# Attention's queries by rotated rows of all heads in one tile, and a norm's row spread by a repeated column

## The chip, the cores and the metric

The kernel runs on one core of a Trainium2 chip. Time is that of the device in microseconds, from the launch to the end on that core. The engines are named as the profile does: PE is TensorE (PEld its weight loads), DVE is VectorE, ACT is ScalarE, POOL is GpSimd, SP is SyncE, which issues nearly all transfers.

## The reference, cut to what matters

The network has two blocks of two layers each, on 512 tokens of width 1024, in float32. Only the first block's token mixer is touched. Each of its two layers projects the tokens into four branches (a short convolution, a gated linear attention, a latent attention and a 31-tap convolution), normalises and joins them. The latent attention computes its queries so:

```python
qm = (rms_norm(cq, g_mla_q) @ w_mla_uq).reshape(bsz, s, MLA_HEADS, MLA_NOPE + MLA_ROPE)
q_c = jnp.concatenate([qm[..., :MLA_NOPE], apply_rope(qm[..., MLA_NOPE:], cos, sin)], axis=-1)
...
k_rope = jnp.broadcast_to(apply_rope(kr[:, :, None, :], cos, sin), (bsz, s, MLA_HEADS, MLA_ROPE))
k_c = jnp.concatenate([kvm[..., :MLA_NOPE], k_rope], axis=-1)

def apply_rope(x, cos, sin):
    x1, x2 = xf[..., :half], xf[..., half:]
    return jnp.concatenate([x1 * c - x2 * s, x1 * s + x2 * c], axis=-1)
```

There are 4 heads, each with 64 plain and 32 rotated columns; the query latent has 256 columns, the key latent 128. The 31-tap branch ends in a layer norm over 256 channels.

## The kernel before, in words

Activations in the mixer lie feature-major: 128 features on the partitions, 512 tokens along a row. Large matmuls are made of three products of float32r halves (`mm3`, lines 368 to 370): weights arrive by transfer as `raw`, ScalarE casts their high half `hi` (line 374), VectorE subtracts it to give `lo` (line 376), and TensorE multiplies hi by hi, hi by lo and lo by hi. Small matmuls, the queries and the scores among them, are plain float32.

`mixers_` loads the layer's constants, projects the latents `cq` (two tiles), `ckv` and `kr`, and in layer 0 makes the angle table `self.trig` (`angles`, lines 580 to 612: integer positions, range reduction on VectorE, a sine on ScalarE, a sign on VectorE). The table holds cosines on partitions 64 to 95 and signed sines on 96 to 127. Lines 709 to 711 rotate the keys' shared row `kr` with it. Layer 1 uses the same table.

Then `merge` interleaves four generators, each with a weight of its own: `linear` (the gated linear attention; its masks are line 923), `mla` (the latent attention), `convolutions` (first the remaining projections of the layer, then 60 multiply-adds per layer in line 784, then a layer norm) and `output`. The program order so written goes to a planner, which simulates a time line with costs of its own and writes each engine's instruction order from it; each engine then runs its own list in order, and waits on semaphores.

`feat_rsqrt` is used for three norms per layer: of `cq`, of `ckv` (both in `mla`, lines 1048 and 1052), and in the 31-tap branch (line 798). `feat_r` gets one number per token: squares, TensorE's sums with a column of ones (line 562), VectorE's scale (line 383), and GpSimd's power (line 384). The four columns `r[:, t]` have tokens on partitions; to spread them along a row over all partitions, VectorE scales the identity's rows by a column (line 573, a diagonal, tile `d`, two buffers) and TensorE multiplies a matrix of ones by it (line 574).

`queries(h)` makes one head's tile from the 128 columns of its weights, which `layout` has put as 64 plain, 32 rotated and the same 32 with their halves exchanged: two matmuls of K = 128 into one PSUM bank (line 1070), a ScalarE copy of the 64 plain rows into `Q` (line 1071), and three VectorE operations on 32 partitions: the rotated rows by the cosines (line 1073), the exchanged rows by the sines (line 1074), and their sum (line 1075). `keys(h)` makes two heads' keys and copies `kr` under each (lines 1081 and 1082). The scores (line 1095) read rows 0 to 95 of `Q` and `K`.

Of the kernel before, what the change touches and what calls it, by code (L numbers as in the profile page):

```python
# [11 lines left out]
F32 = mybir.dt.float32  # L12
# [4 lines left out]
OP = mybir.AluOpType  # L17
# [4 lines left out]
S = 512  # L22
# [33 lines left out]
def stack(units):  # L56
    return np.stack(units)


def cols(v):  # L60

    return v.reshape(-1, 128).T


def rng(a, n):
    return list(range(a, a + n))


def layout(i):
# [11 lines left out]
    for l in range(2):  # L81
        w = f("w_in")[l]
        o = {}
        at = 0
        for n, s in zip(("b", "c", "h", "gq", "gk", "gv", "gg", "gf", "gb", "cq", "ckv", "kr", "cfm"),
                        (256, 256, 256, 128, 128, 256, 256, 16, 16, 256, 128, 32, 512)):
            o[n] = at
            at += s
        kr = rng(o["kr"], 32)
        fm = lambda a: fm_unit(w, rng(a, 128))  # L90
        gvgg = w[:, o["gv"]:o["gv"] + 512]
        units = [fm_unit(w, rng(o["gf"], 32) + [-1] * 32 + kr + kr[16:] + kr[:16]), fm(o["gq"]),
                 fm(o["gk"]), fm(o["cq"]), fm(o["cq"] + 128), fm(o["ckv"])]
        units += [fm(o["cfm"]), fm(o["cfm"] + 256), fm(o["cfm"] + 128), fm(o["cfm"] + 384)]
        units += [tok_units(gvgg, 0, kp) for kp in range(4)]
        for c in range(2):
            units += [fm(o["c"] + 128 * c), fm(o["h"] + 128 * c), fm(o["b"] + 128 * c)]
        A[f"win{l}"] = stack(units)
        uq = f("w_mla_uq")[l]
        q = []  # L100
        for h in range(4):
            r = rng(96 * h + 64, 32)
            q += rng(96 * h, 64) + r + r[16:] + r[:16]
        uq = uq.reshape(2, 128, 384)[:, :, q].reshape(2, 128, 4, 128).transpose(1, 2, 0, 3).reshape(128, 1024)
        kv = f("w_mla_ukv")[l].reshape(128, 4, 128)
        ukv = np.zeros((128, 1024), kv.dtype)
        ukv[:, :256] = kv[:, :, :64].reshape(128, 256)
        ukv[:, 256:512] = kv[:, :, 64:].reshape(128, 256)
        A[f"wmla{l}"] = stack([uq, ukv])
        up = f("w_gla_a_up")[l]  # L110
        wu = np.zeros((32, 256), up.dtype)
        wu[:16, :128] = up[0]
        wu[16:, 128:] = up[1]
        A[f"wgla{l}"] = wu
        wo = f("w_out")[l]
        A[f"wout{l}"] = stack([tok_units(wo, c, kp) for p in ((0, 3), (1, 2)) for c in range(2) for kp in p])
        wup = f("w_ffn_up")[l]
        A[f"wup{l}"] = stack([fm_unit(wup, rng(h * FF + 128 * m, 128)) for m in range(FT) for h in range(2)])
        wd = f("w_ffn_down")[l]
        units, k0 = [], 0  # L120
        for n in FFN_PARTS:
            units += [tok_units(wd, c, kp) for c in range(2) for kp in range(k0 // 2, (k0 + n) // 2)]
            k0 += n
        A[f"wdown{l}"] = stack(units)
        v = [cols(f("b_gla_a")[l].reshape(-1))]
        for c in range(2):
            v.append(f("w_sc_conv")[l][:, 128 * c:128 * c + 128].T)
        v += [cols(f("g_mla_q")[l]), cols(f("g_mla_kv")[l])]
        for c in range(2):
            v.append(f("w_cfm_dw")[l][:, 128 * c:128 * c + 128].T)  # L130
        v += [cols(f("g_cfm_ln")[l]), cols(f("b_cfm_ln")[l]), cols(f("g_branch")[l])]
        v.append(f("w_ffn_dw")[l].reshape(3, 44, 128).transpose(2, 1, 0).reshape(128, 132))
        A[f"vec{l}"] = np.concatenate(v, 1)
        A[f"gh{l}"] = f("g_gla_head")[l][None]
# [4 lines left out]
    for l in range(2):  # L139
        w = f("w_in_2")[l]  # L140
        b = f("b_in_2")[l]
        o = {}
# [117 lines left out]
class Lane:  # L260
# [20 lines left out]
    def s(self, shape, dt=F32):  # L281
        n = int(np.prod(shape[1:]))
        return self.tile(shape, dt, *(("s16", 12) if n <= 16 else ("s64", 4)))

    def d(self):
        return self.tile((128, 128), F32, "d", 2)


class Net:
# [276 lines left out]
    def feat_rsqrt(self, L, sq, n):  # L566

        nc = self.nc
        r = self.feat_r(L, sq, n)
        R = L.P()  # L570
        for t in range(NT):
            d = L.d()
            nc.vector.tensor_scalar(d, self.ident, r[:, t:t + 1], None, op0=OP.mult)
            nc.tensor.matmul(R[:, t * 128:(t + 1) * 128], self.ones, d, start=True, stop=True)
        return R

    def square(self, L, src):
# [63 lines left out]

    def block1_consts(self):
        self.gmask = self.blk.tile([128, 8, 128], U8, name="gmask")
        self.trig = self.blk.tile([128, S], F32, name="trig1")
        self.hmask = self.const("hmask", 256, self.blk)

    def mixers(self, l, x):
# [3 lines left out]
    def mixers_(self, l, x):  # L651
        nc = self.nc
        ve, ac = nc.vector, nc.scalar
        A = Lane(self, "A", ps=2)
        G = Lane(self, "G", ps=2, w=5, v=11)
        M = Lane(self, "M", ps=2, w=7, v=5)
# [18 lines left out]
        ps = fst[0]  # L675
        ga = G.w()
        ac.copy(ga[0:32], ps[0:32])
        kr = M.w()
# [11 lines left out]
        q, k = G.w(), G.w()  # L690
        ps = fst[1]
        ac.activation(q, ps, AF.Copy, scale=32 ** -0.5)
        ps = fst[2]
# [6 lines left out]
        latent = ac.copy(ckv, self.fm(A, st.next(), x))  # L700

        with self.tc.issue_after(last.ins):
            if l == 0:
                raw = self.rawp.tile([128, 1024], F32, tag="raw", name=self.nm("raw"))
                nc.sync.dma_start(raw, self.A["gmask"])
                nc.gpsimd.tensor_copy(self.gmask.rearrange("p a b -> p (a b)"), raw)
                self.angles(M, "pos", 0, 1, 2, self.trig, latent)
            tmp = M.w()
            ve.tensor_tensor(out=tmp[64:96], in0=kr[96:128], in1=self.trig[96:128], op=OP.mult)
            ve.tensor_tensor(out=kr[64:96], in0=kr[64:96], in1=self.trig[64:96], op=OP.mult)  # L710
            ve.tensor_tensor(out=kr[64:96], in0=kr[64:96], in1=tmp[64:96], op=OP.add)

        gv = [G.v() for _ in range(NT)]
# [331 lines left out]
    def mla(self, L, wm, cq, ckv, kr, g_q, g_kv, attended):  # L1045
        nc = self.nc
        ve, ac = nc.vector, nc.scalar
        R = self.feat_rsqrt(L, [self.square(L, a) for a in cq], 256)
# [3 lines left out]
        R = self.feat_rsqrt(L, [self.square(L, ckv)], 128)  # L1052
        ve.scalar_tensor_tensor(ckv, ckv, g_kv, R, op0=OP.mult, op1=OP.mult)
        yield 1
        Q, K = self.g8(), self.g8()
        T = self.trig
        v = []
        for t in range(NT):
            ps = L.P((128, 256))
# [3 lines left out]
            v.append(vt)  # L1063
        yield 1

        def queries(h):
            ps = L.P()
            for k in range(2):
                o = (2 * h + k) * 128
                nc.tensor.matmul(ps, wm[:, 0, o:o + 128], cq[k], start=k == 0, stop=k == 1)  # L1070
            ac.copy(Q[0:64, h], ps[0:64])
            tmp = L.w()
            ve.tensor_tensor(out=Q[64:96, h], in0=ps[64:96], in1=T[64:96], op=OP.mult)
            ve.tensor_tensor(out=tmp[64:96], in0=ps[96:128], in1=T[96:128], op=OP.mult)
            ve.tensor_tensor(out=Q[64:96, h], in0=Q[64:96, h], in1=tmp[64:96], op=OP.add)

        def keys(h):
            ps = L.P()
# [5 lines left out]
        for h in (0, 2):  # L1084
            keys(h)
            yield 1
        for h in range(4):
            queries(h)
            yield 1.7
        PP, PT, O = {}, {}, {}  # L1090

# [1032 lines left out]
```

## Time and profile before

| | |
|---|---|
| time, median of 3 runs (lowest, highest) | 2965.17 us (2964.11, 2965.36) |
| profiled execution: its time, its span | 2962.75 us, 2960.6 us |
| mean granted TensorE clock over the span | 0.983 |
| busy share of the span: PE, DVE, ACT, POOL | 97%, 73%, 48%, 13% |

The profiled execution is one run of its own; the span runs from its first to its last instruction, and the time has some 2 us more around it. The granted clock is a share of TensorE's full 2.4 GHz; 0.5 is its lower level, 1.2 GHz, and a stretch's figure is the mean over it. Busy times of TensorE come from modelled ends of pipelined matmuls.

### The profile page before, as it was taken

The numbers are of one execution on the slowest core, as the hardware profiler recorded it, in microseconds if no ns is written. First come the engines' busy times: TensorE is split into PE (matmuls) and PEld (weight loads), VectorE is DVE, ScalarE is ACT, GpSimd is POOL, SyncE is SP. The second block draws the span as 40 slices with busy tenths as digits, with TensorE's granted clock in tenths as the row PEclk, the third lists the DMA queues.
The fourth block names the chain that finished last, engine by engine and source line by source line (L and its number), as shares of the span: only waits on it lengthen the run. The fifth ranks groups of instructions, "written<-read, shape, count | busy, mean of one in ns | idle before, by whom it ended". The sixth has DMA issues, their size and how long they took to land.

```text
span 2960.6 us, 37914 instructions
## 1 busy us (share of the span) xinstructions
PE 2864.5 (97%) x13982; PEld 2246.9 (76%) x13982; DVE 2167.0 (73%) x3532; ACT 1430.1 (48%) x2214; POOL 372.2 (13%) x359
## 2 busy tenths in 40 slices
PE   7999999999999999999999998999999999989996
PEld 6777888878778888878787786777687777867774
DVE  6998655576978556687876447999768764479997
ACT  4444423335444333335544424888445444238884
POOL 1012000010011000011101002110411011021203
PEclk9999999999999999999999998999999999989998
DMA  5121332332213233343232266999632322669993
GB/s 194 54 90 51 93 97 95 100 128 89 65 58 94 94 99 100 107 154 110 61 97 89 76 253 235 380 384 358 233 92 66 98 76 81 226 240 371 387 381 122
DMA packets 128589, 457.34 MB, mean 154 GB/s; under 512 B 15696, under 2 KB 16912, under 8 KB 126992
## 3 DMA queue, kind: packets, MB, share of 16 engines
q1 hardware_dynamic: 117776, 425.50, 41.5%
q0 software_dynamic: 7168, 16.79, 1.7%
q10 hardware_dynamic: 3456, 12.58, 1.1%
q8 instruction: 112, 1.84, 0.3%
q14 instruction: 77, 0.63, 0.1%
HBM read 429.12 MB, written 27.26 MB: 154 GB/s over the span
## 4 chain that ended last, share of the span: by engine, by line
PE 86%; DVE 10%; ACT 2%; issue 1%; DMA 0%; POOL 0%; POOLq 0%; SPq 0%; DVEq 0%; ACTq 0%
PE AP L368 16%; PE AP L369 16%; PE AP L370 16%; PE HP L370 4%; PE HP L369 4%; PE HP L368 4%; PE BP L370 3%; PE BP L368 3%; PE BP L369 3%; PE YP L370 2%; PE YP L369 2%; PE YP L368 2%; DVE cacc L784 2%; DVE lo L376 2%; PE O L1610 1%
## 5 line engine op out<-in xcount | busy, mean ns | idle before, releaser
L368 PE MATMUL AP<-g,hi 128*128 128x512 f32 (+1 forms) x1856 | 717.8, 388 | 9.7 <-DVE g L886 4.0
L369 PE MATMUL AP<-g,hi 128*128 128x512 f32 (+1 forms) x1856 | 710.8, 383 | 10.6 <-DVE g L376 10.6
L370 PE MATMUL AP<-g,lo 128*128 128x512 f32 (+1 forms) x1856 | 710.7, 383 | 0.0
L376 DVE TENSOR_TENSOR lo<-raw,hi 128x1024 fp32r<-128x1024 f32 x326 | 412.2, 1266 | 359.7 <-ACT hi L374 350.3
L374 ACT CAST hi<-raw 128x1024 fp32r<-128x1024 f32 x326 | 341.8, 1050 | 562.6 <-PE AP L369 380.7
L368 PEld LDWEIGHTS AP<-g,hi 128*128 128x128 f32 x1856 | 353.2, 191 | 80.4 <-DVE g L886 4.9
L369 PEld LDWEIGHTS AP<-g,hi 128*128 128x128 f32 x1856 | 353.6, 191 | 77.6 <-DVE g L376 12.0
L370 PEld LDWEIGHTS AP<-g,lo 128*128 128x128 f32 x1856 | 353.4, 190 | 66.1 <-issue 1.4
L376 DVE TENSOR_TENSOR lo<-g,hi 128x1024 fp32r<-128x1024 f32 x204 | 239.2, 1219 | 23.3 <-ACT hi L374 22.9
L374 ACT CAST hi<-g 128x1024 fp32r<-128x1024 f32 x204 | 207.0, 1051 | 50.2 <-PE AP L370 32.4
L376 DVE TENSOR_TENSOR lo<-wide,hi 128x1024 fp32r<-128x1024 f32 x180 | 212.3, 1225 | 25.1 <-ACT hi L374 23.5
L370 PE MATMUL HP<-hi,Txt 128*96 128x512 f32 x512 | 203.8, 398 | 0.0
L369 PE MATMUL HP<-lo,Txt 128*96 128x512 f32 x512 | 203.2, 397 | 0.2
L368 PE MATMUL HP<-hi,Txt 128*96 128x512 f32 x512 | 200.9, 400 | 1.1 <-ACT Txt L374 1.1
L374 ACT CAST hi<-wide 128x1024 fp32r<-128x1024 f32 x180 | 182.7, 1050 | 21.9 <-PE HP L370 18.7
L368 PE MATMUL AP<-hi,g 128*128 128x512 f32 x400 | 165.8, 418 | 0.3 <-DVE g L886 0.3
L370 PE MATMUL AP<-hi,g 128*128 128x512 f32 x400 | 158.1, 397 | 0.4 <-DVE g L891 0.4
L369 PE MATMUL AP<-lo,g 128*128 128x512 f32 x400 | 157.4, 394 | 0.0
L368 PE MATMUL BP<-hi,g 128*128 128x512 f32 x352 | 136.8, 390 | 0.0
L369 PE MATMUL BP<-lo,g 128*128 128x512 f32 x352 | 136.6, 389 | 0.0
L370 PE MATMUL BP<-hi,g 128*128 128x512 f32 x352 | 134.0, 389 | 0.0
L369 PEld LDWEIGHTS HP<-lo,Txt 128*96 128x96 f32 x512 | 83.4, 163 | 39.2 <-DVE lo L376 2.6
(509 smaller groups left out, 4901.7 us busy)
## 6 DMA issues: line engine op xcount, KB each, us to landing
wide<-in_wmoeu SPq DMA_DIRECT2D x64, 1024.0 KB, 8.4
g<-in_wmoeu SPq DMA_DIRECT2D x64, 1024.0 KB, 8.4
raw<-in_wup SPq DMA_DIRECT2D x88, 512.0 KB, 3.5
g<-in_wmoed SPq DMA_DIRECT2D x34, 1024.0 KB, 9.4
wide<-in_wmoed SPq DMA_DIRECT2D x30, 1024.0 KB, 8.4
raw<-in_xwin SPq DMA_DIRECT2D x50, 512.0 KB, 3.7
raw<-in_xgate SPq DMA_DIRECT2D x48, 512.0 KB, 3.6
raw<-in_wdown SPq DMA_DIRECT2D x44, 512.0 KB, 3.5
```

Source lines behind the costliest of these rows:

```text
L368: mm(ps, a[0], b[0], start=start, stop=False)
L369: mm(ps, a[0], b[1], start=False, stop=False)
L370: self.product = mm(ps, a[1], b[0], start=False, stop=stop)
L374: self.nc.scalar.copy(hi, src)
L376: self.cut = (engine or self.nc.vector).tensor_tensor(out=lo, in0=src, in1=hi.bitcast(F32), op=OP.subtract)
L784: ve.scalar_tensor_tensor(acc, ubs[c][:, j:j + S], w_dw[:, 31 * c + j:31 * c + j + 1], acc, op0=OP.mult, op1=OP.add)
L1610: nc.tensor.matmul(O[j][64 * b:64 * b + 64, t * 128:(t + 1) * 128], v[:, s, c:c + 64], PT[i - 1 + b][:, s, :], start=s == 0, stop=s == t, ...
```

## The change

`layout` puts the columns of the query weights in another order: the plain columns of heads 0 and 1, those of heads 2 and 3, the rotated columns of all four heads, and the same with exchanged halves, 128 each. `queries(i)` makes these groups in the order 2, 3, 0, 1. Groups 2 and 3 are multiplied on all 128 partitions by the cosines and the sines; their sum is copied by ScalarE, 32 rows for each head, into `Q`. Groups 0 and 1 are copied 64 rows at a time.

The angle table becomes two rows of tables on 128 partitions, each with the 32 values repeated four times. `angles` writes into a working tile, and eight transfers on SyncE's queue, 32 partitions of 2 KB each, put the pieces into the table. `kr` is rotated from it.

`feat_rsqrt` gives TensorE the column `r[:, t]`, repeated 128 times by an access pattern with a step of 0, as the loaded operand, and the identity as the moving one. The diagonals and their tile are gone.

```diff
@@ -97,10 +97,9 @@
             units += [fm(o["c"] + 128 * c), fm(o["h"] + 128 * c), fm(o["b"] + 128 * c)]
         A[f"win{l}"] = stack(units)
         uq = f("w_mla_uq")[l]
-        q = []
-        for h in range(4):
-            r = rng(96 * h + 64, 32)
-            q += rng(96 * h, 64) + r + r[16:] + r[:16]
+        turns = [rng(96 * h + 64, 32) for h in range(4)]
+        q = [i for h in range(4) for i in rng(96 * h, 64)]
+        q += [i for r in turns for i in r] + [i for r in turns for i in r[16:] + r[:16]]
         uq = uq.reshape(2, 128, 384)[:, :, q].reshape(2, 128, 4, 128).transpose(1, 2, 0, 3).reshape(128, 1024)
         kv = f("w_mla_ukv")[l].reshape(128, 4, 128)
         ukv = np.zeros((128, 1024), kv.dtype)
@@ -282,9 +281,6 @@
         n = int(np.prod(shape[1:]))
         return self.tile(shape, dt, *(("s16", 12) if n <= 16 else ("s64", 4)))
 
-    def d(self):
-        return self.tile((128, 128), F32, "d", 2)
-
 
 class Net:
     def __init__(self, tc, A, out, ctx, dump=None):
@@ -569,9 +565,8 @@
         r = self.feat_r(L, sq, n)
         R = L.P()
         for t in range(NT):
-            d = L.d()
-            nc.vector.tensor_scalar(d, self.ident, r[:, t:t + 1], None, op0=OP.mult)
-            nc.tensor.matmul(R[:, t * 128:(t + 1) * 128], self.ones, d, start=True, stop=True)
+            nc.tensor.matmul(R[:, t * 128:(t + 1) * 128], r[:, t:t + 1].to_broadcast([128, 128]), self.ident,
+                             start=True, stop=True)
         return R
 
     def square(self, L, src):
@@ -641,7 +636,7 @@
 
     def block1_consts(self):
         self.gmask = self.blk.tile([128, 8, 128], U8, name="gmask")
-        self.trig = self.blk.tile([128, S], F32, name="trig1")
+        self.trig = self.blk.tile([128, 2, S], F32, name="trig1")
         self.hmask = self.const("hmask", 256, self.blk)
 
     def mixers(self, l, x):
@@ -704,10 +699,15 @@
                 raw = self.rawp.tile([128, 1024], F32, tag="raw", name=self.nm("raw"))
                 nc.sync.dma_start(raw, self.A["gmask"])
                 nc.gpsimd.tensor_copy(self.gmask.rearrange("p a b -> p (a b)"), raw)
-                self.angles(M, "pos", 0, 1, 2, self.trig, latent)
+                trig = M.w()
+                self.angles(M, "pos", 0, 1, 2, trig, latent)
+
+                for i in range(2):
+                    for h in range(4):
+                        nc.sync.dma_start(out=self.trig[32 * h:32 * h + 32, i], in_=trig[64 + 32 * i:96 + 32 * i])
             tmp = M.w()
-            ve.tensor_tensor(out=tmp[64:96], in0=kr[96:128], in1=self.trig[96:128], op=OP.mult)
-            ve.tensor_tensor(out=kr[64:96], in0=kr[64:96], in1=self.trig[64:96], op=OP.mult)
+            ve.tensor_tensor(out=tmp[64:96], in0=kr[96:128], in1=self.trig[96:128, 1], op=OP.mult)
+            ve.tensor_tensor(out=kr[64:96], in0=kr[64:96], in1=self.trig[64:96, 0], op=OP.mult)
             ve.tensor_tensor(out=kr[64:96], in0=kr[64:96], in1=tmp[64:96], op=OP.add)
 
         gv = [G.v() for _ in range(NT)]
@@ -1063,16 +1063,22 @@
             v.append(vt)
         yield 1
 
-        def queries(h):
+        def queries(i):
+
             ps = L.P()
             for k in range(2):
-                o = (2 * h + k) * 128
+                o = (2 * i + k) * 128
                 nc.tensor.matmul(ps, wm[:, 0, o:o + 128], cq[k], start=k == 0, stop=k == 1)
-            ac.copy(Q[0:64, h], ps[0:64])
-            tmp = L.w()
-            ve.tensor_tensor(out=Q[64:96, h], in0=ps[64:96], in1=T[64:96], op=OP.mult)
-            ve.tensor_tensor(out=tmp[64:96], in0=ps[96:128], in1=T[96:128], op=OP.mult)
-            ve.tensor_tensor(out=Q[64:96, h], in0=Q[64:96, h], in1=tmp[64:96], op=OP.add)
+            if i < 2:
+                for j in range(2):
+                    ac.copy(Q[0:64, 2 * i + j], ps[64 * j:64 * j + 64])
+                return
+            turned.append(L.w())
+            ve.tensor_tensor(out=turned[-1], in0=ps, in1=T[:, i - 2], op=OP.mult)
+            if i == 3:
+                ve.tensor_tensor(out=turned[0], in0=turned[0], in1=turned[1], op=OP.add)
+                for h in range(4):
+                    ac.copy(Q[64:96, h], turned[0][32 * h:32 * h + 32])
 
         def keys(h):
             ps = L.P()
@@ -1084,8 +1090,9 @@
         for h in (0, 2):
             keys(h)
             yield 1
-        for h in range(4):
-            queries(h)
+        turned = []
+        for i in (2, 3, 0, 1):
+            queries(i)
             yield 1.7
         PP, PT, O = {}, {}, {}
```

## Rows read from the trace of the kernel before

**Rows 1.** The page's first section: busy us, share of the span, instructions.

```profile
PE 2864.5 (97%) x13982; PEld 2246.9 (76%) x13982; DVE 2167.0 (73%) x3532; ACT 1430.1 (48%) x2214; POOL 372.2 (13%) x359
```

**Rows 2.** Busy by stretch: us, PE, PEld, DVE, ACT, POOL; clock, DMA share, GB/s.

```profile
135.00:180.00 45.00, 44.92 (x219) 32.89 (x219) 44.50 (x73) 18.29 (x38) 0.13 (x2) 1.00 0.23 72
180.00:200.00 20.00, 18.66 (x109) 12.96 (x108) 18.58 (x38) 7.12 (x15) 1.44 (x1) 0.85 0.56 211
200.00:290.00 90.00, 89.67 (x510) 67.78 (x508) 73.23 (x171) 46.52 (x99) 19.85 (x24) 0.99 0.10 30
735.00:820.00 85.00, 85.00 (x428) 63.00 (x427) 84.45 (x141) 34.78 (x75) 0.13 (x2) 1.00 0.20 63
820.00:840.00 20.00, 17.32 (x91) 12.70 (x89) 15.88 (x31) 6.61 (x13) 1.01 (x1) 0.66 0.53 202
840.00:920.00 80.00, 79.08 (x457) 60.60 (x456) 64.03 (x154) 39.74 (x88) 14.77 (x19) 1.00 0.09 27
```

**Rows 3.** Chain of waits, 735 to 827 us: shares by engine and line.

```profile
by line: DVE cacc L784 34.3%; DVE lo L376 12.9%; DVE g L923 11.4%; issue 7.9%; DVE Gw L946 3.3%; DVE Mw L1074 3.1%; DVE g L1075 3.0%; DVE g L1073 3.0%; DVE Gw L942 2.6%; DVE Cw L758 2.3%; DVE g L984 2.1%; DVE Gv L720 1.5%; DVE g L966 1.5%; 
```

**Rows 4.** Order of time, 825.5 to 827 us: start, length, instruction.

```profile
826.71 0.57 PE L915 MATMUL GP<-Gw,Gw 32*128 32x128 f32 x1 [2.69 <-DVE g L923]
```

**Rows 5.** Groups of instructions on VectorE, 735 to 826 us.

```profile
L1074 DVE TENSOR_TENSOR Mw<-MP,trig 32x512 f32<-32x512 f32 x4 | 2.8, 696 | 0.1
...
L1073 DVE TENSOR_TENSOR g<-MP,trig 32x512 f32<-32x512 f32 x4 | 2.8, 689 | 0.1
L1075 DVE TENSOR_TENSOR g<-g,Mw 32x512 f32<-32x512 f32 x4 | 2.7, 684 | 0.1
```

**Rows 6.** Order of time on VectorE, 757 to 764 us.

```profile
760.95 0.69 DVE L1073 TENSOR_TENSOR g<-MP,trig 32x512 f32<-32x512 f32 x1
761.65 0.69 DVE L1074 TENSOR_TENSOR Mw<-MP,trig 32x512 f32<-32x512 f32 x1
762.38 0.68 DVE L1075 TENSOR_TENSOR g<-g,Mw 32x512 f32<-32x512 f32 x1
```

**Rows 7.** One line's instructions: line 752; ns minimum, median, maximum.

```profile
L752 DVE TENSOR_TENSOR pad<-AP,Cw x4: 679/684/694, 157.4 to 815.7; 128x512 f32<-128x512 f32 x4
```

**Rows 8.** Order of time on VectorE, 138 to 140.5 us.

```profile
139.07 0.67 DVE L946 TENSOR_TENSOR Gw<-Gw,Gw 128x512 f32<-128x512 f32 x1
139.67 0.41 DVE L968 TENSOR_TENSOR g<-g,g 128x256 f32<-128x256 f32 x1
```

**Rows 9.** One line's instructions and what they waited for: line 573.

```profile
L573 DVE TENSOR_SCALAR Md<-c_ident,Ms x16: 265/280/288, 86.7 to 730.8; 128x128 f32<-128x128 f32 x16
L573 DVE TENSOR_SCALAR Cd<-c_ident,Cs x8: 275/280/288, 204.6 to 847.4; 128x128 f32<-128x128 f32 x8
...
  POOL Cs L384: 2.0, 2
```

**Rows 10.** Order of time, weight loads of TensorE, 138.3 to 139 us.

```profile
138.39 0.19 PEld L370 LDWEIGHTS AP<-g,lo 128*128 128x128 f32 x1
...
138.62 0.19 PEld L368 LDWEIGHTS AP<-g,hi 128*128 128x128 f32 x1
```

**Rows 11.** One line's instructions: the scores, line 1095.

```profile
L1095 PE MATMUL MP<-g,g x64: 590/592/697, 155.8 to 905.2; 96*128 96x512 f32 x64
```

**Rows 12.** One line's instructions: the key copies, line 1082.

```profile
L1082 ACT COPY g<-Mw x8: 608/612/617, 83.8 to 715.5; 32x512 f32<-32x512 f32 x8
```

**Rows 13.** Order of time on VectorE, 76 to 80 us.

```profile
76.61 0.48 DVE L612 TENSOR_SCALAR trig<-trig,c_rconst 128x512 f32<-128x512 f32 x1
...
78.05 0.69 DVE L709 TENSOR_TENSOR Mw<-Mw,trig 32x512 f32<-32x512 f32 x1
```

**Rows 14.** Order of time on SyncE's queue, 1348.9 to 1352 us.

```profile
1348.97 2.41 SPq L1225 DMA_DIRECT2D Bw<-Bw  x4
```

**Rows 15.** Transfers by line: count, KB each, median us to landing.

```profile
Bw<-Bw SPq DMA_DIRECT2D x104, 64.0 KB, 2.0
```

**Rows 16.** Waits on VectorE, whole span: us in total, times, longest us.

```profile
DVE Bw L1226 <- DMA Bw<-Bw: 26.1, 14, 4.3
```

## Prediction, on record before the change was run

> **What bounds the kernel now.** I read the page's first section, then the busy time by stretches in the two mixers (the only code the change touches), then the chain of waits there, then groups and single instructions.
>
> The page [rows 1] names TensorE as the fullest engine, 97%, with VectorE at 73%. That is a mean over the span, so the stretches decide. [rows 2] gives two of each layer: one in which VectorE is full, one in which TensorE is. From 135 to 180 us VectorE is busy 44.5 of 45 us, from 735 to 820 it is 84.45 of 85. After them, from 200 to 290 and from 840 to 920, it falls to 73.2 of 90 and 64.0 of 80, and TensorE stays full. Between the two lies the place where the first kind ends: 180 to 200 and 820 to 840. There TensorE is busy only 18.66 and 17.32 of 20 us, and its granted clock falls to a mean of 0.85 and 0.66, a mixture of 2.4 GHz and 1.2 GHz.
>
> The chain of waits from 735 to 827 [rows 3] runs over VectorE: the 31-tap convolution (cacc), the weights' low halves (lo), the linear branch's masks, and some 3% for each of the three query lines 1073, 1074 and 1075. It ends with TensorE standing 2.69 us for a VectorE mask [rows 4]. So VectorE's work ahead of that point is on the path, and what TensorE loses there is what can be won: time it stood idle, plus time at half clock.
>
> **What can come back.** First layer, 180 to 200: idle 20 - 18.66 = 1.34; clock (1 - 0.85) x 20 = 3.0; together 4.3 us. Second layer, 820 to 840: 2.68 + 0.34 x 20 = 9.5 us [rows 2]. In the VectorE-full stretches themselves TensorE shows no idle time, and its weight loads fill 63.0 of 85 us (74%) against 60.6 of 80 (76%) in the TensorE-bound stretch behind. It is nearly as full in the one as in the other, and I count nothing there.
>
> **The change, part by part**, per mixer layer; there are two.
>
> *Queries, removed.* Four heads with three VectorE operations each, on 32 partitions: four of each line, 2.8, 2.8 and 2.7 us in the second layer's stretch [rows 5], 8.3 together. In order of time they follow one another at steps of 0.70 and 0.73 us [rows 6], so the engine really gives up 12 x 0.7 = 8.4.
>
> *Queries, added.* Two products from PSUM on 128 x 512 and one sum. Not shown as such; nearest is line 752, PSUM times SBUF on 128 x 512: 684 ns [rows 7], no longer than on 32 partitions. From below, a 128 x 512 operation between two others holds the engine for 0.60 [rows 8]. So 1.8 to 2.05; I take 2.0. Net 6.3 us less.
>
> *Norm spread, removed.* Four diagonals for each of three norms, 0.28 us each [rows 9]. The two norms of the queries and of the latent lie ahead of or in the full stretch: 8 x 0.28 = 2.2. The third, the convolution's (Cd), runs after it, where VectorE has room: 4 x 0.28, worth 0 there, 1.1 at most. Added on TensorE: nothing, the same four matmuls per norm, with the column in place of the ones and the identity in place of the diagonal. Whether a repeated column loads slower than a stored tile no row shows. The bounds: no difference, or the 48 loads of line 574 half as long again as the 0.19 us of the loads in [rows 10], 48 x 0.095 = 4.6 us in six places. I take none, since these loads are as large as any other.
>
> Sum for VectorE: 6.3 + 2.2 = 8.5 us per layer.
>
> *Query matmuls.* Same number, other order: both rotated groups first. Head 0 now needs three VectorE operations and copies of all heads instead of its own three; the first scores start at 155.8 us [rows 11] and the first head's chain is not longer than before. No cost.
>
> *ScalarE, added.* The unrotated halves stay four copies. New are four copies of 32 x 512, 0.61 us as those of line 1082 [rows 12]: 2.4 us per layer, on an engine busy 18.3 of 45 us and 34.8 of 85 in these stretches [rows 2]. That spare time hides them. Without that cover they would cost 4.9 in both layers; behind them would wait the casts that feed TensorE's weights.
>
> *First layer only, SyncE and the tables.* Eight copies of 64 KB spread the angle tables. They wait for line 612, which ends at 77.1 us [rows 13], and four such copies take SyncE 2.41 us to issue [rows 14], so eight take 4.8; each lands 2.0 us after its issue [rows 15]: ready at 77.1 + 4.8 + 2.0 = 83.9. Behind them on SyncE stand the next weight loads, held for at most those 4.8 us. On VectorE, lines 709 to 711 wait, which ran from 78.05 [rows 13]; in place they would hold VectorE for 83.9 - 78.05 = 5.9 us, and all queued behind them. The nearest row is the rotary of the second block, the same kind of copy: 26 uses of line 1226 lost 26.1 us in all, 4.3 at worst [rows 16]. So 0 to 5.9, and I take the mean of 1.0. It comes off the first layer's 8.5, and 7.5 is still above the 4.3 to be won there, so it costs nothing in the sum. Who needs the result are the key copies, whose first reader is the first score at 155.8, 72 us later.
>
> **Sum.** VectorE saves 8.5 us per layer; of it counts what TensorE had lost: at most 4.3 in the first layer and 8.5 in the second, 12.8. Idle time comes back with certainty where VectorE is early enough; clock comes back only if the pause that precedes the fall goes altogether. I count the idle in full and 0.7 of the clock: first layer 1.34 + 2.1 = 3.4, second 2.68 + 4.8 = 7.5. Together 10.9 us. The profiled execution took 2962.75 (2960.6 span and 2.1 around it) and would take 2951.9; the median of the three runs is 2.4 above it, so 2965.2 - 10.9 = 2954.3.
>
> **Rivals.**
>
> *The whole saving passes.* If TensorE had room inside the full stretches, 2 x 8.5 = 17 us: 2948. For it: TensorE's busy share is a poor witness, being drawn from modelled ends, and small waits stand between its matmuls. Against: its weight loads are about as dense as where TensorE itself is the bound. The Trainium skill bears on it: "Perfetto Trace Analysis", section "Identifying the Most-Contended Engine", takes the share of weight loads, not of matmuls, as TensorE's measure, and by it TensorE has 26% left at 74%, so that the whole saving would pass. The trace qualifies that: back to back, loads of 0.19 us start every 0.23 [rows 10], which is 83% and not 100.
>
> *Nothing moves.* TensorE's queue is rearranged: the order on all engines comes from a planner which sees other durations, and leaves a pause of the same size where the convolution ends. For it: TensorE's work is unchanged and it is busy over 98% of the four long stretches [rows 2], so any gain must come out of two places of 20 us. Against: the pause there is for VectorE [rows 4], which will be there 8.5 us sooner. 2965, within 0.2%.
>
> *VectorE stands for the tables.* If the eight copies went one behind the other, each with its 2.0 us [rows 15], they would be ready at 77.1 + 16 = 93.1, and with line 709 left in its place VectorE would stand 15.0 us, 6.5 more than the first layer saves. The change would then give 7.5 - 6.5 = 1.0 us: 2964. Against: four copies issued in 2.41 us [rows 14] do not wait for one another, and the planner may put other work first. The Trainium skill speaks for it and against this part of the change: "DMA: Bandwidth & Descriptors", section "Rules for kernel authors", says to join many small transfers into a large one, since below 64 KB one pays mostly overhead. The 2.0 us for 64 KB agrees with that page; that eight of them add up no row shows.
>
> *Slower: TensorE stands for GpSimd.* The diagonal was a buffer: VectorE waited for GpSimd's power (2.0 us at two places) [rows 9], TensorE only for the diagonal. Now the spread matmul itself waits, at the head of TensorE's queue, at six places (three norms, two layers); behind it stand ready projections. Price at each: 1.0 us, and where the clock falls after it another 3.0 as after the pause of 180 to 200. All six would cost 24, which with the gain gives 2965 - 11 + 24 = 2978; at five it is 9 us over, and from there on it is slower. At four it is within 0.2%. Against: a pause of 1 us alone need not bring the clock down, and the planner can put projections ahead of the wait.
>
> **Chances and range.** Forecast, 2948 to 2959: 0.45. The whole saving passes, 2944 to 2949: 0.14. Nothing moves, 2959 to 2971: 0.22. The tables, there too: 0.04. Slower, above 2971: 0.15. A change of 0.2%, 5.9 us, is about what a measurement of this kernel can tell from none. So faster 0.59, same 0.26, slower 0.15. The range reaches over most of the two neighbours: 2945 to 2970; the top also takes in the ScalarE copies uncovered with little gained, the bottom the whole saving and the 2.2 us of the third norm's diagonals.
>
> **What would show it.** Right: VectorE's busy time about 18 us less in the mixers (some 17 ahead of the two points, 2 behind); line 573 gone; three 128 x 512 operations of about 0.68 per layer; the convolution's end some 7 us sooner in each layer; TensorE's clock near 1.0 there; the first feed-forward starting 3 to 4 us sooner, the second about 11. Wrong: TensorE waiting at line 574 for GpSimd, VectorE at line 709 for a DMA, or a new fall of the clock anywhere before 300 or between 690 and 930 us. If the convolution ends sooner and the feed-forward starts no sooner, TensorE was the bound all along.

## The result, and the profile after

The changed kernel took 2984.22 us (median of 6 runs, 2982.73 to 2985.57), the kernel before 2964.50 beside it (6 runs): a ratio of 1.0069, 95% interval 1.0059 to 1.0079. It is slower by some 20 us. The prediction, 2954.3 with a range to 2970, was wrong, and on the wrong side.

What the change does to the instructions is there. The page's first section of the changed kernel, to be held against [rows 1]:

```profile
PE 2873.5 (96%) x13982; PEld 2254.7 (76%) x13982; DVE 2151.6 (72%) x3490; ACT 1436.0 (48%) x2222; POOL 372.6 (12%) x359
```

VectorE has 42 instructions and 15.4 us less. The three new operations on 128 partitions, here as one-line views of the changed kernel, take what those on 32 took [rows 5], and the spread's repeated column loads in the time of a stored tile [rows 10], with no idle time of TensorE before it:

```profile
L1077 DVE TENSOR_TENSOR Mw<-MP,trig x4: 686/692/695, 137.1 to 777.1; 128x512 f32<-128x512 f32 x4
L1079 DVE TENSOR_TENSOR Mw<-Mw,Mw x2: 681/688/694, 143.5 to 779.7; 128x512 f32<-128x512 f32 x2
L568 PEld LDWEIGHTS MP<-c_ident,Ms x32: 185/190/192, 101.8 to 749.4; 128*128 128x128 f32 x32
```

Now the stretches of the changed kernel (columns as in [rows 2]). First come the two places where the prediction looked for its gain, in the second layer the one 20 us later, since that layer starts 19.2 us later; then the stretches behind:

```profile
180.00:200.00 20.00, 20.00 (x130) 15.19 (x128) 14.66 (x27) 8.07 (x15) 1.01 (x1) 1.00 0.36 128
840.00:860.00 20.00, 19.04 (x133) 13.91 (x131) 15.37 (x33) 10.40 (x20) 2.70 (x3) 1.00 0.51 185
...
200.00:220.00 20.00, 17.37 (x93) 13.81 (x92) 14.47 (x39) 12.36 (x24) 2.68 (x3) 0.81 0.20 83
220.00:240.00 20.00, 20.00 (x102) 16.36 (x103) 10.42 (x30) 6.00 (x19) 5.66 (x7) 0.85 0.00 1
280.00:300.00 20.00, 13.84 (x81) 9.80 (x80) 15.02 (x31) 9.18 (x17) 7.69 (x7) 0.86 0.08 27
300.00:320.00 20.00, 16.60 (x72) 14.39 (x69) 9.98 (x16) 4.97 (x7) 3.64 (x4) 0.63 0.27 83
```

At 180 TensorE is full and at 2.4 GHz, where it had 18.66 of 20 us at 0.85; the pause of the second layer has shrunk too. So the predicted gain came, where it was predicted. The loss lies behind: from 200 to 240 the clock falls, and from 280 to 320 TensorE stands and falls again. The kernel before in these four slices (from 300.6 on it is past the mixer):

```profile
200.00:220.00 20.00, 20.00 (x133) 16.76 (x132) 17.78 (x50) 12.23 (x29) 4.80 (x5) 0.97 0.00 1
220.00:240.00 20.00, 20.00 (x114) 14.36 (x115) 14.59 (x44) 11.31 (x30) 5.61 (x8) 1.00 0.00 1
280.00:300.00 20.00, 16.47 (x99) 13.71 (x98) 17.97 (x31) 8.02 (x12) 8.98 (x9) 0.91 0.36 109
300.00:320.00 20.00, 20.00 (x169) 19.96 (x168) 9.89 (x13) 7.87 (x12) 0.94 (x1) 1.00 0.19 53
```

Idle time is the slice less TensorE's busy time, and time lost to the clock is the slice times what its mean lacks of 1. Against the kernel before, the changed kernel has 2.6 us more idle and 6.2 more of clock from 200 to 240, and 6.0 and 8.4 more from 280 to 320.

The mixers in one row each, kernel before and then changed kernel, from the first product of the tile GP to the first transposition of the feed-forward part (BP):

```profile
26.30:300.60 274.30, 267.81 (x1501) 207.77 (x1499) 228.10 (x432) 129.19 (x254) 33.48 (x45) 0.97 0.23 76
668.50:936.50 268.00, 263.27 (x1501) 205.60 (x1500) 218.55 (x414) 125.70 (x250) 29.81 (x41) 0.97 0.22 71
```

```profile
27.60:320.50 292.90, 278.41 (x1499) 217.45 (x1499) 219.64 (x407) 132.22 (x258) 33.85 (x45) 0.92 0.23 72
687.70:958.60 270.90, 261.73 (x1500) 203.51 (x1499) 210.83 (x395) 128.56 (x254) 31.85 (x43) 0.98 0.22 71
```

The first mixer is 18.6 us longer, the second 2.9. In the first, idle time of TensorE rises from 274.30 - 267.81 = 6.5 to 14.5 us, and the time lost to the lower clock from 0.03 x 274.3 = 8.2 to 0.08 x 292.9 = 23.4 (the two-digit clock makes each uncertain by 1.4). Lost TensorE time is thus the whole of it; the four slices above, less the 4.3 us that came back at 180 to 200, give 18.9. More than half of it is the clock.

In the second layer the gain came and was lost again at the mixer's end. The changed kernel there, then the kernel before, whose layer began 19.2 us earlier:

```profile
920.00:940.00 20.00, 15.44 (x96) 10.90 (x94) 17.34 (x37) 10.09 (x20) 8.87 (x9) 0.98 0.07 21
940.00:960.00 20.00, 17.41 (x101) 14.81 (x102) 9.98 (x17) 5.34 (x8) 3.73 (x4) 0.76 0.30 91
```

```profile
900.00:920.00 20.00, 20.00 (x106) 14.99 (x105) 16.45 (x35) 8.14 (x16) 4.21 (x7) 1.00 0.07 25
920.00:940.00 20.00, 18.88 (x133) 16.20 (x132) 18.30 (x33) 8.69 (x14) 9.29 (x9) 1.00 0.45 136
```

Where the first layer loses it shows in the order of time. On VectorE of the changed kernel, the sixth step of attention is normalised:

```profile
212.55 0.48 DVE L1107 TENSOR_SCALAR Mw<-Mw,Ms 128x512 f32<-128x512 f32 x1
```

Its transposition on TensorE could start at 213.0. It starts at 228.34:

```profile
211.44 1.26 PE L1102 MATMUL MP<-g,g 96*128 96x512 f32 x2 [2.63 <-ACT Mw L1040]
212.50 1.06 PE L1020 MATMUL GP<-g,g 128*128 128x256 f32 x2
213.35 1.81 PE L1023 MATMUL GP<-Gv,g 128*128 128x64 f32 x8
...
218.48 2.98 PE L558 MATMUL AP<-ones,Cw 128*128 128x1 f32 x14
221.32 0.77 PE L365 MATMUL AP<-lo,g 128*128 128x512 f32 x1
...
228.34 0.49 PE L1112 MATMUL T<-c_ident,Mw 128*128 128x128 f32 x3
```

TensorE did not wait for it: it was busy with what stands ahead in its list, the linear branch's outputs (L1020, L1023), the convolution's norm (L558) and the first products of the output (L364 to L366), partly at half clock. So the delay is not the list's alone. Just before, TensorE stood 2.63 us for an exponential of attention on ScalarE (L1040, the first row), and the clock then costs 6.8 us from 200 to 240 (0.81 and 0.85). In the kernel before the same step is transposed at 213.14:

```profile
213.14 0.60 PE L1105 MATMUL T<-c_ident,Mw 128*128 128x128 f32 x4
```

Attention is a chain of 16 steps (score, maximum, exponential, normalising, transposition, product), and the mixer can't end before it. Some fifteen microseconds late, its last steps have nothing left to run beside them. The three longest waits of TensorE from 180 to 325 in the changed kernel (us in total, times, longest), then the longest of the kernel before:

```profile
PE T L1112 <- DVE Mw L1107: 4.5, 1, 4.5
PE AP L364 <- DVE g L886: 2.9, 1, 2.9
PE MP L1102 <- ACT Mw L1040: 2.6, 1, 2.6
```

```profile
PE AP L368 <- DVE g L886: 3.4, 2, 3.2
```

The first of these, TensorE standing for the last step of attention, is the mark to look for below; the kernel before has none in its first mixer, though it too stands at the mixer's end, for a sum of the output on VectorE (L886). In the second layer, from 835 to 960 in the changed kernel and from 820 to 960 in the kernel before, the mark has 4.7 us against 0.9:

```profile
PE T L1112 <- DVE Mw L1107: 4.7, 1, 4.7
```

```profile
PE T L1105 <- DVE Mw L1100: 0.9, 1, 0.9
```

### The profile page after: what moved, and what is told of

It is laid out like the page before. It is cut to its first block, busy times and chain, and to the rows that moved or that the text cites. A ratio compares the mean times of both kernels' runs of the same rounds, so it can differ in the third digit from the quotient of the medians.

```text
span 2983.4 us, 37900 instructions
## 1 busy us (share of the span) xinstructions
PE 2873.5 (96%) x13982; PEld 2254.7 (76%) x13982; DVE 2151.6 (72%) x3490; ACT 1436.0 (48%) x2222; POOL 372.6 (12%) x359
## 4 chain that ended last, share of the span: by engine, by line
PE 90%; DVE 5%; ACT 2%; issue 1%; POOL 1%; DMA 0%; POOLq 0%; SPq 0%; DVEq 0%; ACTq 0%
PE AP L364 17%; PE AP L365 17%; PE AP L366 17%; PE HP L366 4%; PE HP L365 4%; PE HP L364 4%; PE BP L365 3%; PE BP L366 3%; PE BP L364 3%; PE YP L366 2%; PE YP L365 2%; PE YP L364 2%; PE GP L915 1%; PE O L1617 1%; DVE lo L372 1%
## 5 line engine op out<-in xcount | busy, mean ns | idle before, releaser
L364 PE MATMUL AP<-g,hi 128*128 128x512 f32 (+1 forms) x1856 | 719.3, 388 | 11.8 <-DVE g L886 3.4
L366 PE MATMUL AP<-g,lo 128*128 128x512 f32 (+1 forms) x1856 | 711.9, 384 | 0.0
L364 PEld LDWEIGHTS AP<-g,hi 128*128 128x128 f32 x1856 | 354.6, 191 | 81.8 <-DVE g L886 4.3
L366 PEld LDWEIGHTS AP<-g,lo 128*128 128x128 f32 x1856 | 354.9, 191 | 67.1 <-issue 1.9
L366 PE MATMUL HP<-hi,Txt 128*96 128x512 f32 x512 | 203.4, 397 | 0.0
L364 PE MATMUL HP<-hi,Txt 128*96 128x512 f32 x512 | 200.4, 399 | 1.1 <-ACT Txt L370 1.1
L364 PE MATMUL AP<-hi,g 128*128 128x512 f32 x400 | 167.4, 422 | 0.0
L366 PE MATMUL AP<-hi,g 128*128 128x512 f32 x400 | 160.6, 404 | 0.0
L364 PE MATMUL BP<-hi,g 128*128 128x512 f32 x352 | 136.8, 389 | 0.0
L366 PE MATMUL BP<-hi,g 128*128 128x512 f32 x352 | 134.0, 389 | 0.0
```

Of the source, the lines that this page charges most:

```text
L364: mm(ps, a[0], b[0], start=start, stop=False)
L366: self.product = mm(ps, a[1], b[0], start=False, stop=stop)
```

## The experiments

Theory A: the loss is in the order. The planner, given other durations, writes another list for TensorE, in which products of the convolution and of the output stand ahead of attention's steps; attention comes late and ends alone. The rivals are named in the expectations. A weight in the interleaving, or a dead addition, moves the lists of all engines together, so TensorE's list was in no run varied alone. Each ratio is to runs of the kernel before made beside that run; the mixers' lengths are of one profiled execution each, and one list can differ there by 6 us (w35 and wl35_43, last section). "Thousand columns" counts what TensorE streams, by its list, ahead of a step's transposition.

| kernel | turns 10 to 16, first layer, thousand columns | mixer 1, 2, us | time, us | ratio to before, 95% interval |
|---|---|---|---|---|
| before | 322 334 343 355 365 376 387 | 274.3, 268.0 | 2964.50 | |
| changed | 341 355 365 376 385 394 394 | 292.9, 270.9 | 2984.22 | 1.0069 (1.0059 to 1.0079) |
| n_only | 322 334 343 355 365 376 387 | 271.8, 270.2 | 2961.97 | 0.9990 (0.9981 to 0.9999) |
| t_calc | 338 352 362 373 385 394 394 | 281.4, 275.5 | 2979.29 | 1.0051 (1.0037 to 1.0064) |
| bw25 | 338 352 362 373 385 394 394 | 281.3, 274.8 | 2976.95 | 1.0046 (1.0032 to 1.0060) |
| w35 | 322 334 343 355 365 376 387 | 268.6, 265.0 | 2955.85 | 0.9978 (0.9968 to 0.9987) |
| a_pad | 322 334 343 355 365 376 387 | 270.8, 260.3 | 2952.55 | 0.9955 (0.9941 to 0.9969) |
| dve_cut | 322 334 343 355 365 376 387 | 271.5, 269.9 | 2966.06 | 1.0006 (0.9997 to 1.0015) |
| w43 | 303 315 325 336 353 364 374 | 273.5, 262.9 | 2958.19 | 0.9979 (0.9970 to 0.9988) |
| bw43 | 317 329 337 348 362 373 383 | 277.3, 272.0 | 2972.05 | 1.0022 (1.0011 to 1.0033) |
| pad1 | 338 352 362 373 385 394 394 | 284.4, 270.9 | 2976.19 | 1.0046 (1.0033 to 1.0060) |
| pad3 | 338 352 362 373 385 394 394 | 287.7, 262.2 | 2970.72 | 1.0025 (1.0015 to 1.0035) |
| pad8 | 338 352 362 373 385 394 394 | 285.3, 266.7 | 2972.87 | 1.0034 (1.0021 to 1.0046) |
| wl35_43 | 322 334 343 355 365 376 387 | 274.7, 266.5 | 2954.72 | 0.9973 (0.9963 to 0.9984) |

**One part alone (n_only).** The kernel before, with the new spread.

```diff
-            d = L.d()
-            nc.vector.tensor_scalar(d, self.ident, r[:, t:t + 1], None, op0=OP.mult)
-            nc.tensor.matmul(R[:, t * 128:(t + 1) * 128], self.ones, d, start=True, stop=True)
+            nc.tensor.matmul(R[:, t * 128:(t + 1) * 128], r[:, t:t + 1].to_broadcast([128, 128]), self.ident,
+                             start=True, stop=True)
```

> The kernel before with one part of the change alone: the norms' rows spread by the repeated column instead of diagonals. Theory A (the list): the loss lies in the order in which TensorE's instructions stand. In the changed kernel the turns of attention's steps 5 to 8 in the first layer stand 7, 14, 17 and 19 thousand streamed columns later in TensorE's list than before, behind products of the convolution and of the output, and the last two steps stand at the list's end with nothing between them; in this kernel the turns from the eighth on stand where they stood before. A expects no loss: 2957 to 2966 us. Rival B (the tables: eight copies and a wait for them, in the first layer) is absent here: also 2957 to 2966. Rival C (TensorE stands at the spread products for GpSimd's rows, the slower case of the prediction): 2972 to 2984.

2961.97 us: no loss. TensorE standing at the spread for GpSimd, the prediction's slower case, is out.

**No table copies (t_calc).** The changed kernel, with both tables computed in place; the small table of constants that `angles` reads, not shown, is laid out to match.

```diff
-                trig = M.w()
-                self.angles(M, "pos", 0, 1, 2, trig, latent)
-                for i in range(2):
-                    for h in range(4):
-                        nc.sync.dma_start(out=self.trig[32 * h:32 * h + 32, i], in_=trig[64 + 32 * i:96 + 32 * i])
+                self.angles(M, "pos", 0, 4, None, self.trig[:, 0], latent)
+                self.angles(M, "pos", 0, None, 2, self.trig[:, 1], latent)
```

> The changed kernel without the eight table copies and the extra working tile: both tables are computed on all 128 partitions, once each, in the first layer. TensorE's list holds attention's turns from the seventh on within 3 thousand columns of the changed kernel's. Theory A (the list): still 2976 to 2986 us. Rival B (the copies and the tables' lateness cost the time in the first layer, the only one that has them): 2960 to 2970, most of the 20 us back. Rival C (GpSimd's rows): unchanged, 2980 to 2986.

2979.29 us, as A expected. The first mixer got 11.5 us back, but the second, which has no copies in either kernel, lost 4.6. B had most of the 20 us come back, and 5 did; pad1 below has the copies and is no slower than this run.

**Order alone, made worse (bw25).** The kernel before; no instruction differs.

```diff
-        merge((linear(), 31), (self.mla(M, wm, cq, ckv, kr, g_q, g_kv, attended), 29), (convolutions(), 112),
+        merge((linear(), 31), (self.mla(M, wm, cq, ckv, kr, g_q, g_kv, attended), 25), (convolutions(), 112),
```

> The kernel before, with one number changed: attention's weight in the interleaving of the four branches, 29 to 25. No instruction is added, removed or made longer; in the first layer the last seven turns of attention stand in TensorE's list at 338, 352, 362, 373, 385, 394 and 394 thousand columns, which is within 3 thousand of the changed kernel (341, 355, 365, 376, 385, 394, 394), where the kernel before has 322, 334, 343, 355, 365, 376, 387. Theory A (the list): slower than before by 8 to 22 us, 2973 to 2987. Rivals B and C, and any theory in which the new instructions themselves cost the time: no change, 2962 to 2968.

2976.95 us, 14 above the kernel before beside it (2963.23), of the changed kernel's 20. Both mixers are 7 us longer, with the changed kernel's mark at the end of the first, in TensorE's waits from 240 to 325 (the second mixer has it too, 3.2 us):

```profile
PE T L1105 <- DVE Mw L1100: 3.2, 1, 3.2
PE AP L368 <- DVE g L886: 3.0, 1, 3.0
...
```

**Order alone, made better (w35).** The same line of the changed kernel with 35 for 29.

> The changed kernel with one number changed: attention's weight in the interleaving, 29 to 35. All the change's instructions are there, tables, copies and spreads too; only the order differs, and from the tenth turn on TensorE's list of the first layer is that of the kernel before (322, 334, 343, 355, 365, 376, 387 thousand columns). Theory A (the list): the 20 us come back and some of the saved VectorE time shows: 2948 to 2965. Rivals B and C: 2976 to 2986.

2955.85 us: 28 us come back, with all of the change's instructions in place. The mark is gone, and the stretches at the convolution's end and at the mixer's end read:

```profile
180.00:200.00 20.00, 20.00 (x138) 15.16 (x136) 14.88 (x28) 8.53 (x19) 0.00 (x0) 1.00 0.21 62
280.00:300.00 20.00, 18.88 (x133) 16.20 (x133) 18.29 (x33) 8.57 (x13) 9.45 (x9) 1.00 0.36 109
300.00:320.00 20.00, 20.00 (x151) 19.09 (x150) 13.22 (x18) 9.32 (x13) 0.50 (x1) 1.00 0.30 88
```

**VectorE's work given back (a_pad).** The changed kernel with dead additions.

```diff
                 ve.tensor_tensor(out=turned[0], in0=turned[0], in1=turned[1], op=OP.add)
+                for _ in range(9):
+                    ve.tensor_tensor(out=turned[1], in0=turned[0], in1=turned[1], op=OP.add)
```

> The changed kernel with nine more VectorE additions of 128x512 per layer, put behind the addition of the turned rows; nothing reads what they write. VectorE's work in attention's front is so about what it was before the change. In TensorE's list the turns from the tenth on stand at 322, 334, 343, 355, 365, 376 and 387 thousand columns in the first layer, as in the kernel before. Theory A (the list; that VectorE is shorter only tipped it): faster than the changed kernel although it does more, 2958 to 2968 us. Rival (the changed instructions cost the time, or VectorE's work is what counts): 2984 to 2995, the added work on top of the changed kernel's.

2952.55 us, below the range: the changed kernel is made 32 us faster by useless work, some 6.3 us of VectorE's in each layer.

**VectorE's work taken from the kernel before (dve_cut).**

```diff
             ve.tensor_tensor(out=Q[64:96, h], in0=ps[64:96], in1=T[64:96], op=OP.mult)
-            ve.tensor_tensor(out=tmp[64:96], in0=ps[96:128], in1=T[96:128], op=OP.mult)
-            ve.tensor_tensor(out=Q[64:96, h], in0=Q[64:96, h], in1=tmp[64:96], op=OP.add)
```

> The kernel before with VectorE's second product and the addition left out of every head's turn of the queries, eight operations per layer (so the queries' turned rows lack one part of the rotation); no tables, copies or new spread. In TensorE's list the turns from the eighth on stand where they stand before. Theory A (the list): the saved VectorE time shows, 2950 to 2962 us. Rival D (whatever shortens VectorE's work in the convolution lets the convolution's products go ahead of attention on the chip, in any list): 2972 to 2985.

2966.06 us, a miss for both. VectorE being shorter did not of itself push attention back here; nor did it win anything. TensorE's pause at the convolution's end went here too, as these stretches show, but the one at the mixer's end stayed:

```profile
180.00:200.00 20.00, 19.87 (x135) 14.38 (x134) 16.48 (x32) 8.66 (x18) 1.01 (x1) 1.00 0.56 198
...
280.00:300.00 20.00, 16.48 (x105) 14.03 (x104) 16.23 (x28) 7.97 (x12) 9.47 (x9) 0.91 0.33 109
```

**Attention further ahead (w43, bw43).** Weight 43 in the changed kernel and in the kernel before.

> The changed kernel with attention's weight in the interleaving 29 to 43. The last seven turns stand in TensorE's list of the first layer at 303, 315, 325, 336, 353, 364 and 374 thousand columns, some 13 thousand earlier than in the kernel before, so that attention is ahead where the changed kernel had it behind. Theory A (the list): at least as good as weight 35 (measured 2955.85), 2943 to 2957 us. Rival E (the list only matters where attention ends last; once it doesn't, nothing more is won, and what is taken from the convolution early is lost): 2955 to 2968.

> The kernel before with attention's weight 29 to 43, to tell how much of what the changed kernel wins at another weight is the change's own. Its last seven turns stand at 317, 329, 337, 348, 362, 373 and 383 thousand columns, 4 to 7 thousand earlier than at 29. Theory A (the list): 2955 to 2964 us, and 5 to 11 us above the changed kernel at the same weight, which is what the shorter VectorE work is then worth. If the change is worth nothing, the two are the same within 4 us.

2958.19 and 2972.05 us. The first is 1 us above A's range and within E's: neither w35 nor w43 has the mark in its first mixer, and the further lead of w43 has won nothing. The second is a clear miss for A as I had put it: the kernel before gets slower although its steps stand earlier. TensorE waits 4.0 us in its second layer for a low half that VectorE makes (L376), and 2.1 for a step of attention. So the positions of the last steps are not a full measure of a list.

**One to eight dead additions (pad1, pad3, pad8).** As in a_pad, with other counts.

> The changed kernel with one dead VectorE addition per layer where the kernel with nine had them. In TensorE's list the last seven turns of both layers stand where the run without table copies had them: 338, 352, 362, 373, 385, 394, 394 thousand columns in the first. Theory A (the list): no recovery, 2976 to 2987 us; if it is near 2979, as the run without table copies (2979.3), the list's early part and not the copies made the 5 us between that and the changed kernel (2984.2); if it is above 2982, the copies did. Rival F (VectorE's load in attention's front works by itself and evenly, 3.5 us for each added operation from 2984.2 to 2952.6): 2980.7.

> The changed kernel with three dead additions per layer. The list is split: in the first layer the last turns stand as in the slow lists (338, 352, 362, 373, 385, 394, 394), in the second as in the fast run with nine (its last seven turns within a thousand columns). Theory A (the list): the profile has the first mixer at 278 to 293 us from its first product to the feed-forward part (270.8 with nine, 293.0 in the changed kernel) and the second at 258 to 265 (260.3 and 270.9); 2962 to 2975 in all. Rival F (evenly by added operations): both mixers a third of the way, about 285.6 and 267.4, 2973.7 in all.

> The changed kernel with eight dead additions per layer, one fewer than in the run that was fastest (2952.55). The first layer's list is again a slow one (338, 352, 362, 373, 385, 394, 394 thousand columns), the second's last seven turns stand as with nine. Theory A (the list): one operation fewer costs the first mixer 8 to 20 us: 278 to 291 us, the second 258 to 265; 2960 to 2973 in all. Rival F (evenly by added operations): first mixer 273, 2956 in all.

2976.19, 2970.72 and 2972.87 us. F fails: nine additions give 2952.55 and eight 2972.87. The time goes with the list, layer by layer: in pad3 the first mixer, with a late list, has 287.7 us, and the second, with an early one, 262.2 (F expected 267.4). In pad8 they have 285.3 and 266.7, the latter 1.7 above A's range. One operation more, and this is what changes between 280 and 320, pad8 first and then a_pad:

```profile
280.00:300.00 20.00, 14.91 (x79) 11.71 (x78) 11.47 (x25) 8.09 (x15) 4.67 (x5) 0.76 0.09 27
300.00:320.00 20.00, 17.30 (x126) 16.59 (x125) 12.05 (x17) 5.06 (x7) 3.10 (x3) 0.90 0.25 83
```

```profile
280.00:300.00 20.00, 18.86 (x128) 15.88 (x127) 18.59 (x31) 9.18 (x14) 8.65 (x8) 1.00 0.36 108
300.00:320.00 20.00, 20.00 (x158) 19.38 (x157) 12.96 (x18) 9.97 (x15) 1.35 (x1) 1.00 0.23 77
```

TensorE's waits in the same place, 240 to 325, of pad8; a_pad has no line for T:

```profile
PE T L1114 <- DVE Mw L1109: 3.2, 1, 3.2
```

pad1 has the eight copies and is 3 us below t_calc, which has none: the copies cost nothing that shows, though the two differ also by a dead addition and by t_calc's second computation of the angles.

**A weight for each layer (wl35_43).** The changed kernel with `(35, 43)[l]`.

> The changed kernel with attention's weight 35 in the first layer and 43 in the second, the better of the two in each layer by the profiles (first mixer 268.6 at 35 and 273.6 at 43, second 265.0 and 262.9). Theory A (the list): 267 to 272 and 259 to 265 us for the mixers, 2946 to 2956 in all, faster than both kernels with no dead work. If the choice by layer does not carry over (the second layer's list also turned with the first's weight): 2955 to 2960, as at one weight.

2954.72 us, faster than both kernels with no dead work. But its profile does not bear out the reason: the second mixer has 266.5 us, not 259 to 265, and the first 274.7, though TensorE's list there is w35's instruction for instruction. Its eight runs lie in two groups, five from 2953 to 2955 and three from 2959 to 2961, and the profiled one is of the upper.

## Why the prediction was wrong

- *VectorE's saving*: right in kind and nearly in size. In the two mixers VectorE has 16.2 us less (15.4 over the span), against some 18. The last multiply-add of the second layer's convolution (L784) starts at 839.1, not 832.3, in a layer that begins 19.2 later, so 12.4 sooner than before; that of the first layer at 181.7, not 194.9, in a layer that begins 1.3 later, so 14.5 sooner; against "some 7". Both are more than the 8.5 us that VectorE was to save per layer, so here too the order changed, and not only the durations.
- *The pauses at the convolution's end*: right. They went or shrank, 4.3 us in the first layer, and 8.5 of 9.5 in the second. The prediction's "clock comes back only if the pause that precedes the fall goes altogether" was not borne out there: 0.96 us of idle time are left from 840 to 860, at a clock of 1.00.
- *Spread, ScalarE copies, tables*: right at nothing. L568 has no idle time of TensorE, n_only is not slower, pad1 and w35 carry the copies and tables. VectorE has no wait for a DMA from 60 to 100 us. The prediction left open, beside the Trainium skill ("DMA: Bandwidth & Descriptors", "Rules for kernel authors", against many small transfers), whether eight copies add up. The page's advice decides nothing here: 2976.19 with them (pad1), 2979.29 without (t_calc).
- *The step that failed* is the sum: "of it counts what TensorE had lost", idle in full and 0.7 of the clock, together 10.9 us. It takes for granted that what TensorE does behind the pause stays in its order and moves up. The planner wrote another list, in which attention's last seven turns stand 7 to 22 thousand columns later in the first layer. The loss at the convolution's end went, and larger ones came behind it. At the mixer's end, where attention runs alone, the first layer has 6.0 us more idle and 8.4 more of clock than before (280 to 320), and the second layer stands 4.7 us for attention's last step. From 200 to 240 the first layer has another 2.6 and 6.2.
- *The rival "nothing moves"* named the agent, a planner that sees other durations, but left its pause where the convolution ends and gave it the old size. Of the prediction's signs of being wrong one came, "a new fall of the clock anywhere before 300": 0.81 from 200 to 220. No rival had it at the mixer's end, nor that a list could be worse than the one it replaces.
- Even with a good list the saving was not shown to be what wins. a_pad puts 18 operations of 0.7 us back into VectorE's list and is the fastest; dve_cut takes 10.8 us from VectorE over the span (2167.0 to 2156.2) and measures 1.0006. What the saving is worth with the list held fixed could not be tried, since each duration that is changed makes a new list.

Shown: that a change of order alone, with every instruction as it was, makes a loss of this kind (bw25, 14 us) and undoes the changed kernel's (w35, 28 us). That the loss sits in attention's late end is borne out by the mark: it stands in the first mixer of the changed kernel, t_calc, bw25, pad1, pad3 and pad8 (281 to 293 us), and in none of the other eight (269 to 277 us). It is no full account, since bw43 is slow without it. Open: the other lists with the mark lose 7 to 13 us in the first mixer, and the changed kernel itself 18.6. Its sixth turn stands at 293 thousand columns, where pad1 has 285, and it spends more time at the lower clock, from 212 on and again at the end. That the one makes the other, and both the further 5 to 12, was not tried alone; nor do single executions tell how much of that clock is the list's doing. Open too is what in the durations tips the planner: one dead addition did.

## What to carry over

Where a planner writes the engines' order, a cheaper instruction is a new order first and a saving second; compare the lists before counting a saving, and ask which chain ends the stage and what is left to run beside its last links. A change that comes out on the wrong side should be tried again at one or two other weights of the interleaving before it is dropped: here the same instructions measure 2984 at 29 and 2956 at 35. And a time that moves by 20 us for one dead operation says that differences below that, between two planned kernels, are not yet differences between their instructions.

## What the runs showed of the hardware

- The same list can meet another clock. The first layer's TensorE list is the same in w35 and wl35_43; the mixer took 268.6 and 274.7 us with a mean granted clock of 0.99 and 0.96, which is some 3 and 11 us lost at the lower level of 1.2 GHz (each uncertain by 1.4). VectorE's and ScalarE's lists are the same there too. From 200 to 220 TensorE is busy 18.68 us in both, at 1.00 in the one and at 0.74 in the other. The rows, w35 and then wl35_43:

```profile
27.70:296.30 268.60, 263.72 (x1500) 204.55 (x1499) 216.67 (x406) 131.13 (x257) 31.30 (x43) 0.99 0.24 76
200.00:220.00 20.00, 18.68 (x120) 14.47 (x119) 16.56 (x46) 11.94 (x25) 4.38 (x5) 1.00 0.38 151
```

```profile
27.80:302.50 274.70, 269.95 (x1500) 208.55 (x1500) 216.76 (x405) 131.11 (x257) 31.27 (x43) 0.96 0.23 75
200.00:220.00 20.00, 18.68 (x92) 13.49 (x91) 12.71 (x34) 7.05 (x16) 2.65 (x3) 0.74 0.42 163
```

  The Trainium skill ("TensorE: Matmul & The Clock Gate", "Part 1: The HAM clock gate") says something near it of a kernel's start: there one kernel meets different numbers of slow matmuls from run to run. No run here bears on the start; these two differ inside the kernel.
- A column repeated by a step of 0 loads into TensorE in 190 ns (L568), as a stored 128 x 128 tile does [rows 10], and VectorE takes 0.69 us for a product of 512 columns whether 32 partitions work [rows 5] or 128 (L1077).
